# A mixer layer and sixteen experts on one core: another beginning, other fill-in steps, weight slots taken over in halves, another grouping of the last experts

## The chip, the cores and the metric

The program runs on one core of a Trainium2 chip: one TensorE (PE), VectorE (DVE), ScalarE (ACT), GpSimd (POOL), SyncE (SP) and sixteen DMA engines. The metric is device microseconds of one execution. Queues that issue DMAs are written SPq and ACTq.

## The reference

One layer on x of 512 tokens by 1024, all in float32:

```python
h = rms_norm(x, norm_mix_g)
z = h @ w_in                                   # 5648 columns
y_a = mlstm_branch(z, ...) @ w_up_a            # 4 heads, forward and backward scans, conv of width 5
y_b = diff_attention_branch(z, ...) @ w_up_b   # 4 heads, two softmaxes each
x = x + (g_a * y_a + g_b * y_b) @ w_out        # g_a, g_b: sigmoids of columns of z
h2 = rms_norm(x, norm_ffn_g)
x = x + expert_choice_ffn(h2, ...)             # 16 experts; each takes its 64 best tokens
return rms_norm(x, norm_f_g)
```

An expert is `(silu(xe @ w_gate) * (xe @ w_up)) @ w_down`, scaled by the token's affinity and added to the rows it took. Its three matrices are 1024 by 2048, 8.4 MB each, 403 MB for the sixteen.

## The kernel before

**The trunk** is everything up to the router. x comes in four tiles of 128 tokens. Each is squared on ACT (line 266) and scaled to xs; PE transposes xs into hps, ACT and DVE split it into a high part hH and a low part hL, and each product of the trunk is three float32r matmuls (lines 310 to 312), from which zps comes. The weight columns come in "heads" of 512 KB, named raw, which ACT, DVE and POOL split into two parts, sp. The first two are DQ and DK. Six small vectors (norm gains, the convolution) are loaded as rows of one tile, prow, which PE transposes to pc; a mult by pc stands in hH's evacuation and in the router's weights wr.

**What sets the order.** PE, and at the start ACT and DVE, run in the order in which the code is written (`manual_schedule`). POOL's and SP's rows are put in order by the scheduler of the language. A DMA is issued by the engine whose name stands before `dma_start`, in the order of that engine's instructions. After the matmuls of z come four mLSTM heads, in which steps of other work are run between the steps of a head ("fill-in"): for heads 0 and 1 the projections q and k of a later head, for heads 2 and 3 the generator `gate_b`, which makes the gated up-projection of the attention branch. In a head, pn are the matmuls with the scan's state, and DVE makes the row `first` that they read (line 599) and rsq (line 129).

**The experts.** The weights go through a ring of eleven slots of 2 MB (`NSLOT`), one DMA on SP for a piece of 2 MB, or two for halves of 1 MB. PIECES lists the pieces in their order; a new piece takes the slot of an older one as soon as PE has read that. A few slots are kept and not handed on (`_slots`): one holds mats (the one-hot matrices of the scatter, oa and oaT, and the results yb), one the sums acc, one the gain of the last norm. The first 23 half pieces are issued without a wait for PE, as soon as the trunk's tiles leave their space.

Expert e's passes: gate, then the down of the expert before, then up. `gather` makes xe of two experts at a time: one-hot matmuls into pg (line 1034). Two experts also share a scatter: `scatter_mats` makes the one-hot matrices (line 1047, POOL), transposes the affinities and the matrices (pa at line 1053, pt at line 1064), and `scatter` adds the results to the sums in eight passes, pg at line 1151, laid between the matmuls of another expert's up. pgate and pup are the banks of gate and up (line 1083), pd that of down (line 1167). The experts are paired (0,1) to (12,13); 14 goes alone (`no_odd`), and 15, the last, scatters nothing: its rows of the sums are picked out by one-hot matmuls px (line 1225), with pi for their numbers, its 64 rows are finished apart, and an indirect store (line 1255) writes them over out, behind four stores of the other rows (line 1245).

Of the kernel before, what the change touches and what calls it, by code (L numbers as in the profile page):

```python
# [19 lines left out]
P = 128  # L20
# [51 lines left out]
def kernel(  # L72
# [60 lines left out]
    def rsqrt_act(dst, ssq, scale, pool):  # L133
        w = pool.tile([P, 3, 4], F32, tag="rsq", name="rsq", bufs=4)
        v, u = w[:, 0, 0:dst.shape[-1]], w[:, 1, 0:dst.shape[-1]]
        ve.tensor_scalar(v, ssq, scale, EPS, op0=OP.mult, op1=OP.add)
        se.activation(u, v, AF.Sqrt)
        ve.reciprocal(dst, u)
        ve.tensor_mul(u, dst, dst)
        ve.tensor_mul(u, u, v)  # L140
        ve.tensor_scalar(u, u, -0.5, 1.5, op0=OP.mult, op1=OP.add)
        ve.tensor_mul(dst, dst, u)

# [52 lines left out]
    first_sqrt = consts.tile([P, 1], F32, name="first_sqrt")  # L196
    se.activation(first_sqrt, ident[:, 0:1], AF.Sqrt)
    prow = gt("prow", (NROW, P))
    sy.dma_start(prow[0:8], norm_mix_g[0].rearrange("(k p) -> k p", p=P))
    sy.dma_start(prow[8:16], norm_ffn_g[0].rearrange("(k p) -> k p", p=P))  # L200
    sy.dma_start(prow[16:24], conv_b[0].rearrange("(k p) -> k p", p=P))
    sy.dma_start(prow[24:64], conv_w[0].rearrange("w (k p) -> (w k) p", p=P))
    sy.dma_start(prow[64:68], mlstm_norm_g[0].rearrange("(k p) -> k p", p=P))
    sy.dma_start(prow[68:69], diff_norm_g[0:1])
# [57 lines left out]
    ss = r4.tile([P, 2, NT], F32, name="ss")  # L262
    xs = []
    for t in range(NT):
        xs.append(st_("xs", (P, D)) if t < 3 else r4.tile([P, D], F32, tag="mqk", name="xs", bufs=2))
        se.activation(xs[t], xt[t], AF.Square, accum_out=ss[:, 0, t:t + 1])
        if t % 2 == 1:
            rsqrt_act(ss[:, 1, t - 1:t + 1], ss[:, 0, t - 1:t + 1], 1.0 / D, consts)
            for i in (t - 1, t):
                if i == 2:  # L270
                    se.activation(xs[i], xt[i], AF.Copy, scale=ss[:, 1, i:i + 1])
                else:
                    ve.tensor_scalar(xs[i], xt[i], ss[:, 1, i:i + 1], None, op0=OP.mult)
# [3 lines left out]
    for ks in (range(ND - 1), range(ND - 1, ND)):  # L277
        for t in range(NT):
            for k in ks:
                pe.transpose(hps[k][:, t * P:(t + 1) * P], xs[t][:, k * P:(k + 1) * P], ident)  # L280
# [4 lines left out]
    pre[0] = sq  # L285
    for k in range(ND):
        last_evac = split_evac(hT(hH, k), hT(hL, k), hps[k], pc[:, G_MIX + k:G_MIX + k + 1])
# [425 lines left out]
    for h in range(H):  # L713
        head = mlstm_head(h)
        more = steps(lambda: mlstm_q(h + 2), lambda: mlstm_k(h + 2)) if h < 2 else gate_b
        for i, (n, m) in enumerate(((2, 2), (2, 1), (1, 1), (1, 2))):
            run(head, n)
            if (h, i) == (0, 1):
                attn_out(3)
            run(more, m)  # L720
# [253 lines left out]
    def slot_for(*key):  # L974
        n = npiece[0]
        assert PIECES[n] == key
        npiece[0] += 1
        if not NSLOT <= n < NHALVES:
            ring[SLOT_OF[n]] = mw.tile([P, 4096], F32, tag=f"w{SLOT_OF[n]}", name="w")
        return ring[SLOT_OF[n]]  # L980

    def in_halves():

        return NSLOT < npiece[0] <= NHALVES

# [32 lines left out]
    ga = consts.tile([P, 2, 1], F32, name="ga")  # L1018
    fs = consts.tile([P, 6, NT], F32, name="fs")
# [21 lines left out]
    def scatter_mats(p):  # L1041


        for t in range(NT):
            for j, q in enumerate((0, 1, 0)):
                e = 2 * p + q
# [22 lines left out]
    def first_mats():  # L1069
# [3 lines left out]
        yield from scatter_mats(0)  # L1073
# [13 lines left out]
    def up_pass(e, m, tag, ahead, behind):  # L1087
# [65 lines left out]
    def down(e, behind=nothing):  # L1153
# [4 lines left out]
        for q in range(4):  # L1158
            wt = slot_for(e, "down", q)
            src = w_down_e[0, e, q * 512:(q + 1) * 512, :].rearrange("(p i) d -> p (i d)", i=4)  # L1160
            n = 1 if (e, q) == (LAST, 3) else 2 if in_halves() else 4
            for i in range(0, 4, n):
                sy.dma_start(wt[:, i * D:(i + n) * D], src[:, i * D:(i + n) * D])
            for i in range(4):
                c = 4 * q + i
                for s, h in enumerate(order):
                    pe.matmul(pd[s * 64:(s + 1) * 64], hid_col(q, i), wt[:, i * D + h * 512:i * D + (h + 1) * 512],  # L1167
# [8 lines left out]
    def scatter(p):  # L1176
# [3 lines left out]
        for e in range(2):  # L1180
            es = slice(e * 512, (e + 1) * 512)
            for t in range(NT):
                pq = pgt((P, 512))
                scatter_mm(pq, e, t, es)
# [5 lines left out]
    def no_odd():  # L1190

        for s in range(2):
            gp.memset(yb[s * 64:(s + 1) * 64, :, (1 - s) * 512:(2 - s) * 512].bitcast(F32), 0.0)
        yield

    def others():

        for _ in range(3):
            yield
        for t in range(NT):  # L1200
            a = accs[t]
            for h in range(2):
                hs = slice(h * 512, (h + 1) * 512)
                pq = pgt((P, 512))
                scatter_mm(pq, h, t, hs)
# [8 lines left out]
    def last_rows():  # L1214

        gp.iota(tokc, pattern=[[256, NT], [1, 2]], base=0, channel_multiplier=2, allow_small_or_imprecise_dtypes=True)
        gp.tensor_tensor(pair.rearrange("p (a b) -> p a b", a=2), ident[:, 0:64].unsqueeze(1).broadcast_to([P, 2, 64]),
                         ident[:, 64:128].unsqueeze(1).broadcast_to([P, 2, 64]), op=OP.add)
        for s in range(2):
            gp.tensor_copy(gh[s * 64:(s + 1) * 64], gf[s * 64:(s + 1) * 64, s * 512:(s + 1) * 512])  # L1220
        yield
        own = [oa[:, t, CAP:2 * CAP].bitcast(F32) for t in range(NT)]
        for t in range(NT):
            for s in range(2):
                pe.matmul(px[s * 64:(s + 1) * 64, 0], own[t], accs[t][:, s * 512:(s + 1) * 512],
                          start=(t == 0), stop=(t == NT - 1))
            yield
        se.activation(xg, px[:, 0], AF.Copy)
        pi = pm.tile([P, 2], F32, tag="pt", name="pi", bufs=1)
        for s in range(2):  # L1230
            for t in range(NT):
                pe.matmul(pi[s * 64:(s + 1) * 64], own[t], tokc[:, t], start=(t == 0), stop=(t == NT - 1))
        for s in range(2):
            ve.tensor_copy(idx[s * 64:(s + 1) * 64], pi[s * 64:(s + 1) * 64, s:s + 1])
        yield
        for t in range(NT):
            a, r = accs[t], fs[:, 2, t:t + 1]
            gp.tensor_mul(a[:, 0:512], a[:, 0:512], gf[:, 0:512])
            se.activation(a[:, 0:512], a[:, 0:512], AF.Copy, scale=r)
            ve.scalar_tensor_tensor(a[:, 512:1024], a[:, 512:1024], r, gf[:, 512:1024], op0=OP.mult, op1=OP.mult)  # L1240

    def last_end(pd):
# [3 lines left out]
        ve.scalar_tensor_tensor(y, pd, ga[:, 1], xg, op0=OP.mult, op1=OP.add)  # L1246
        se.activation(sq[:, 0], y, AF.Square, scale=1.0 / 32.0, accum_out=fs[:, 5, 0:1])
# [15 lines left out]
    for e in range(NE):  # L1263
# [5 lines left out]
        else:  # L1269
            pg = up_pass(e, "gate", "pgate", nothing if e % 2 else gather(e // 2),  # L1270
                         others() if e == LAST else chain(hid_T(), scatter_mats(b // 2) if e % 2 and e > 1 else nothing))
        se.activation(sg, pg.rearrange("p a b -> p (a b)"), AF.Silu)  # L1272
        if e == LAST:
            px = pm.tile([P, 2, 512], F32, tag="pgate", name="px", bufs=1)
            pair, tokc = mats[:, 3968:4096], ohr[:, 0, 0:2 * NT].rearrange("p (t c) -> p t c", c=2)
            idx = ohr[:, 1, 0:1].bitcast(I32)
# [50 lines left out]
```

## Time and profile before

| | us |
|---|---|
| median of three runs | 1370.09 |
| lowest and highest | 1367.3, 1371.68 |
| the profiled execution | 1370.63 |
| its span | 1368.3 |
| PE busy | 1301.3 (95%) |
| DVE, ACT, POOL busy | 415.5, 304.5, 131.1 |
| DMA moved | 444.02 MB, mean 325 GB/s |

The profile is of one execution. Its times start at the span's start. Busy time is counted by engine; a wait is the idle time of an engine just before an instruction, put down to what released it. The slices of the page are 34.2 us each. The granted clock of PE is 1.00 at full speed.

### The profile page before, as it was taken

The page shows a single profiled execution, that of the slowest core. Times are in us where ns is not written, and L with a number is a line of the kernel's source. Part 1 is how long each engine was busy: PE and PEld are TensorE (multiplying, and loading weights), DVE is VectorE, ACT ScalarE, POOL GpSimd, SP SyncE. Part 2 cuts the span into 40 slices and gives each one's busy share as a digit, 9 for nine tenths or more (in the row PEclk, how much of TensorE's full clock was granted, in tenths as well). Part 3 has the DMA queues.
Part 4 walks back from the last instruction along what each step waited for, and adds up shares of the span by engine and source line. Part 5 has one row for each costly group of instructions (what it writes and reads, how often), then busy time and mean ns, then how long its engine had stood idle before and what let it go on. Part 6 is the DMA issues. An engine that isn't in the chain of part 4 may idle for free.

```text
span 1368.3 us, 16140 instructions
## 1 busy us (share of the span) xinstructions
PE 1301.3 (95%) x6566; PEld 711.8 (52%) x6566; DVE 415.5 (30%) x982; ACT 304.5 (22%) x621; POOL 131.1 (10%) x239
## 2 busy tenths in 40 slices
PE   8999999999999999999999998999899899889997
PEld 8988897888888534433433432423333242333332
DVE  5687759853443211020030020111102012010241
ACT  7676646433331010100000001000010000001030
POOL 3010212200111011000000000000000000000020
PEclk9999999999999999999999999999999999999999
DMA  7223242223478899999999999999999999999996
GB/s 205 64 64 89 81 109 62 63 77 107 134 280 344 339 425 427 427 428 427 429 428 427 428 427 428 427 428 428 428 427 429 428 427 427 427 428 427 428 427 276
DMA packets 81737, 444.02 MB, mean 325 GB/s; under 512 B 6353, under 2 KB 49431, under 8 KB 54656
## 3 DMA queue, kind: packets, MB, share of 16 engines
q1 hardware_dynamic: 79312, 438.43, 78.6%
q10 hardware_dynamic: 2240, 4.25, 1.3%
q8 instruction: 51, 0.84, 0.2%
q0 software_dynamic: 112, 0.33, 0.1%
q14 instruction: 22, 0.18, 0.0%
HBM read 440.58 MB, written 2.38 MB: 324 GB/s over the span
## 4 chain that ended last, share of the span: by engine, by line
PE 69%; DMA 22%; DVE 4%; issue 3%; ACT 2%; POOL 0%; POOLq 0%; SPq 0%; ACTq 0%; DVEq 0%
DMA w<-in_w_up_e_dram 21%; PE pgate L1083 14%; PE pup L1083 12%; PE pd L1167 7%; PE pg L1034 4%; PE zps L310 4%; PE zps L312 4%; PE zps L311 4%; PE pg L1151 3%; PE pt L1129 1%; PE bank L784 1%; PE bank L786 1%; PE bank L785 1%; PE pa L1053 1%; PE zps L352 1%
## 5 line engine op out<-in xcount | busy, mean ns | idle before, releaser
L1083 PE MATMUL pup<-w,xe 128*64 128x512 f32 x1024 | 240.1, 600 | 27.1 <-DMA w<-in_w_up_e_dram 27.1
L1083 PE MATMUL pgate<-w,xe 128*64 128x512 f32 x1016 | 243.7, 603 | 0.7 <-ACT sh L1272 0.7
L1167 PE MATMUL pd<-w,sh 128*64 128x512 f32 x1024 | 228.5, 597 | 15.4 <-DMA w<-in_w_down_e_dram 13.6
L1167 PEld LDWEIGHTS pd<-w,sh 128*64 128x64 f32 x1024 | 71.2, 137 | 162.6 <-issue 130.8
L1083 PEld LDWEIGHTS pup<-w,xe 128*64 128x64 f32 x1024 | 69.1, 136 | 165.4 <-issue 115.9
L1083 PEld LDWEIGHTS pgate<-w,xe 128*64 128x64 f32 x1016 | 63.0, 136 | 98.5 <-issue 85.2
L1146 DVE SCALAR_TENSOR_TENSOR mats<-pd,ga,mats 64x512 fp32r<-64x512 f32 x30 | 22.5, 750 | 289.1 <-ACT mats L1144 288.6
L310 PE MATMUL zps<-hH,sp 128*128 128x512 f32 x256 | 101.9, 398 | 0.8 <-DVE hL L234 0.8
L312 PE MATMUL zps<-hH,sp 128*128 128x512 f32 x256 | 100.0, 391 | 0.0
L311 PE MATMUL zps<-hL,sp 128*128 128x512 f32 x256 | 99.9, 390 | 0.0
L250 DVE TENSOR_TENSOR sp<-raw,sp 128x512 fp32r<-128x512 f32 x114 | 78.1, 688 | 54.6 <-ACT sp L249 52.0
L1034 PEld LDWEIGHTS pg<-ohr,xn 128*128 128x128 f32 x512 | 64.8, 196 | 45.4 <-issue 44.6
L249 ACT ACTIVATE sp<-raw 128x512 fp32r<-128x512 f32 x114 | 70.9, 630 | 69.5 <-PE zps L620 27.6
L1034 PE MATMUL pg<-ohr,xn 128*128 128x128 f32 x512 | 75.8, 293 | 0.2 <-DVE ohr L1027 0.2
L1284 DVE TENSOR_TENSOR sh<-sh,pup 128x512 f32<-128x512 f32 x32 | 20.6, 684 | 140.2 <-PE pup L1083 133.3
L1144 ACT ACTIVATE mats<-pd,ga 64x512 fp32r<-64x512 f32 x30 | 20.5, 683 | 191.6 <-PE pd L1167 191.3
L1038 ACT ACTIVATE xe<-pg,gff 128x128 f32<-128x128 f32 x32 | 11.8, 368 | 228.8 <-PE pg L1034 228.8
L1133 ACT ACTIVATE sh<-pt 128x512 f32<-128x512 f32 x16 | 9.6, 598 | 237.6 <-PE pt L1129 237.6
L1047 POOL TENSOR_SCALAR mats<-iota,slot 128x64 fp32r<-128x64 f32 x64 | 26.8, 444 | 313.4 <-PE pt L1064 288.2
L310 PEld LDWEIGHTS zps<-hH,sp 128*128 128x128 f32 x256 | 48.1, 188 | 10.6 <-POOL sp L284 1.0
L312 PEld LDWEIGHTS zps<-hH,sp 128*128 128x128 f32 x256 | 48.1, 188 | 10.4
L311 PEld LDWEIGHTS zps<-hL,sp 128*128 128x128 f32 x256 | 48.1, 188 | 9.5
(337 smaller groups left out, 1551.8 us busy)
## 6 DMA issues: line engine op xcount, KB each, us to landing
w<-in_w_down_e_dram SPq DMA_DIRECT2D x59, 2048.0 KB
w<-in_w_gate_e_dram SPq DMA_DIRECT2D x56, 2048.0 KB
w<-in_w_up_e_dram SPq DMA_DIRECT2D x56, 2048.0 KB
raw<-in_w_in_dram SPq DMA_DIRECT2D x44, 512.0 KB
w<-in_w_up_e_dram SPq DMA_DIRECT2D x16, 1024.0 KB
w<-in_w_gate_e_dram SPq DMA_DIRECT2D x15, 1024.0 KB
w<-in_w_down_e_dram SPq DMA_DIRECT2D x8, 1024.0 KB
raw<-in_w_out_dram SPq DMA_DIRECT2D x8, 512.0 KB
```

The costliest lines, as they stand in the source:

```text
L249: se.activation(sp[:, 0], raw, AF.Copy)
L250: ve.tensor_sub(sp[:, 1], raw, sp[:, 0].bitcast(F32))
L310: pe.matmul(zp, w[:, 1], hT(hH, k), start=(k == 0), stop=False)
L311: pe.matmul(zp, w[:, 0], hT(hL, k), start=False, stop=False)
L312: pe.matmul(zp, w[:, 0], hT(hH, k), start=False, stop=(k == ND - 1))
L1034: pe.matmul(pg, xn[t][:, c0:c0 + 255:2], ohr[:, t], start=(t == 0), stop=(t == NT - 1))
L1047: (gp if j else ve).tensor_scalar(oa[:, t, j * CAP:(j + 1) * CAP], iota, slot[:, t, e:e + 1], None, op0=OP.is_equal)
L1083: pe.matmul(pu[s * 64:(s + 1) * 64, c], xe[:, b, half:half + CAP], wt[:, c0:c0 + 512], start=(b == 0), stop=(b == ND - 1))
L1146: ve.scalar_tensor_tensor(yb[r, 1, c], src[r], ga[r, e % 2], yb[r, 0, c].bitcast(F32), op0=OP.mult, op1=OP.subtract)
L1151: pe.matmul(pq, oaT[:, v, t], yb[:, i, cols], start=(i == 0), stop=(i == 1))
L1167: pe.matmul(pd[s * 64:(s + 1) * 64], hid_col(q, i), wt[:, i * D + h * 512:i * D + (h + 1) * 512], start=(c == 0), stop=(c == 15))
L1284: ve.tensor_mul(sg[:, cols], sg[:, cols], pu[:, i])
```

## The change

Four edits. **The beginning:** the six loads of prow go from SP to ACT; SP issues DQ and DK right behind x; the table that ACT loads first is that of Exp; the reciprocal roots of the norm are made on POOL with pow; DVE takes half of a Square; the work on x goes by tiles. **The fill-in:** heads take 2, 2, 1, 1 steps, and gate_b follows where q and k have run out. **Half slots:** `OVER` lists the pieces of 1 MB that go into slots already in use, half by half: the last gate block of expert 1, the down of expert 0 and the up of expert 1; mats is kept in the first slot of these. **The last passes:** 12 is scattered alone, 13 goes with 14, and the matrices for that, own, pair and pi are made beside the down of 12, in another kept slot, "last".

```diff
 EXTRA = (0, "gate", 7)
 BLOCKS.remove(EXTRA)
+OVER = BLOCKS[2 * NSLOT:] + [(0, "down", b) for b in range(8)] + [(1, "up", b) for b in range(8)] + [None]
+BLOCKS = BLOCKS[:2 * NSLOT] + OVER
...
-    keep = {(0, "down", 0): "mats", (1, "down", 3): "acc", (12, "gate", 0): "gf"}
+    keep = {PIECES[NSLOT]: "mats", (1, "down", 3): "acc", (12, "gate", 0): "gf", (12, "gate", 1): "last"}
...
-    sy.dma_start(prow[0:8], norm_mix_g[0].rearrange("(k p) -> k p", p=P))
...
+    se.dma_start(prow[0:8], norm_mix_g[0].rearrange("(k p) -> k p", p=P))
+    se.dma_start(prow[8:16], norm_ffn_g[0].rearrange("(k p) -> k p", p=P))
+    se.dma_start(prow[16:24], conv_b[0].rearrange("(k p) -> k p", p=P))
+    se.dma_start(prow[24:64], conv_w[0].rearrange("w (k p) -> (w k) p", p=P))
+    se.dma_start(prow[64:68], mlstm_norm_g[0].rearrange("(k p) -> k p", p=P))
+    se.dma_start(prow[68:69], diff_norm_g[0:1])
+    pre = [load_head(c) for c in (DQ, DK)]
     graw = gt("graw", (P, ND, NGATE))
     sy.dma_start(graw, wi[:, MG:MG + NGATE].rearrange("(k p) c -> p k c", p=P))
-    pre = [load_head(c) for c in (DQ, DK)]
...
+    def rms(t0, t1):
+
+        v = ss[:, 0, t0:t1]
+        gp.tensor_scalar(v, v, 1.0 / D, EPS, op0=OP.mult, op1=OP.add)
+        gp.tensor_tensor(ss[:, 1, t0:t1], v, ss[:, 3, t0:t1], op=OP.pow)
...
+    se.activation(xs[3][:, 0:512], xt[3][:, 0:512], AF.Square, accum_out=ss[:, 0, 3:4])
+    ve.tensor_tensor_reduce(xs[3][:, 512:], xt[3][:, 512:], xt[3][:, 512:], 1.0, 0.0, op0=OP.mult, op1=OP.add,
+                            accum_out=ss[:, 2, 3:4])
+    gp.tensor_add(ss[:, 0, 3:4], ss[:, 0, 3:4], ss[:, 2, 3:4])
+    rms(3, 4)
...
-        more = steps(lambda: mlstm_q(h + 2), lambda: mlstm_k(h + 2)) if h < 2 else gate_b
-        for i, (n, m) in enumerate(((2, 2), (2, 1), (1, 1), (1, 2))):
+        more = [gate_b] if h > 1 else [steps(lambda: mlstm_q(h + 2), lambda: mlstm_k(h + 2)), gate_b]
+        for i, (n, m) in enumerate(((2, 2), (2, 2), (1, 1), (1, 1))):
...
-            down(b, nothing if b else first_mats())
+            down(b, last_mats() if b == LAST - 3 else nothing if b else first_mats())
...
-                         last_rows() if e == LAST else scatter(b // 2) if b % 2 else nothing)
+                         first_rows() if e == LAST else scatter(b // 2) if b % 2 and b < LAST - 2 or b == LAST - 3
+                         else nothing)
```

On ACT, the first instructions of the program before. DMAHW with a number is a semaphore of a DMA queue, the others are those of the engines; x_63, x_65, x_67 and x_69 are the four tiles of x.

```order
L760 DMA gff<-in_norm_ffn_g_dram 128x4x2
L197 ACT_TABLE_LOAD
L197 ACTIVATE first_sqrt<-ident 128x1 [waits Pool_49]
L266 ACTIVATE xs,ss<-x_63 128x1024 [waits DMAHW1_49]
L266 ACTIVATE xs,ss<-x_65 128x1024 [waits DMAHW2_49]
L137 ACTIVATE rsq<-rsq 128x2 [waits DVE_49]
L266 ACTIVATE xs,ss<-x_67 128x1024 [waits DMAHW3_49]
L266 ACTIVATE xs,ss<-x_69 128x1024 [waits DMAHW4_49]
```

And after:

```order
L187 ACTIVATE first_exp<-ident 128x1 [waits Pool_49]
L189 DMA prow<-in_norm_mix_g_dram 8x128
L190 DMA prow<-in_norm_ffn_g_dram 8x128 [waits DMAHW0_49]
L191 DMA prow<-in_conv_b_dram 8x128 [waits DMAHW2_49]
L192 DMA prow<-in_conv_w_dram 40x128 [waits DMAHW4_49]
L193 DMA prow<-in_mlstm_norm_g_dram 4x128 [waits DMAHW6_49]
L194 DMA prow<-in_diff_norm_g_dram 1x128 [waits DMAHW0_49]
L271 ACTIVATE xs,ss<-x_63 128x1024 [waits DMAHW1_49]
L271 ACTIVATE xs,ss<-x_65 128x1024
L273 ACTIVATE xs,ss<-x_67 128x1024 [waits DMAHW3_49]
L279 ACTIVATE xs,ss<-x_69 128x512
```

Six issues stand ahead of the first Square, five with a wait. DMAHW1 to DMAHW4 are, after as before, those of x's four tiles, DMAHW5 and DMAHW6 those of the heads DQ and DK; DMAHW0 is that of gff and then of a row of prow.

On POOL, at the same place, from the split of the first head on, before:

```order
L284 TENSOR_TENSOR sp<-raw,sp 128x512 [waits DMAHW4_49,Activation_49]
L284 TENSOR_TENSOR sp<-raw,sp 128x512 [waits Activation_49]
L303 TENSOR_SCALAR wr<-wr,pc 128x16 [waits DMASW0_49,DVE_49]
L303 TENSOR_SCALAR wr<-wr,pc 128x16 x7
L450 MEMSET first_305 64x512 [waits Pool_49]
L450 MEMSET first_305 64x512
L470 IOTA first_304 128x896 [waits Pool_49]
```

And after; ss holds the sums of squares and the roots:

```order
L287 TENSOR_TENSOR sp<-raw,sp 128x512 [waits DMAHW5_49,Activation_49]
L313 TENSOR_SCALAR wr<-wr,pc 128x16 [waits DMASW0_49,DVE_49]
L313 TENSOR_SCALAR wr<-wr,pc 128x16 x7
L460 MEMSET first_299 64x512 [waits Pool_49]
L460 MEMSET first_299 64x512
L480 IOTA first_298 128x896 [waits Pool_49]
L282 TENSOR_TENSOR ss<-ss 128x1 [waits DVE_49]
L460 MEMSET qk 64x512 [waits Pool_49]
L258 TENSOR_SCALAR ss<-ss 128x1 [waits Pool_49]
L460 MEMSET qk 64x512
L259 TENSOR_TENSOR ss<-ss 128x1 [waits Pool_49]
```

The last three rows of ss belong to x tile 3; they stand behind wr, the memsets of first and an iota.

On PE, the last matmuls of the program, before:

```order
L1225 MATMUL px<-acc,mats 64x512 x2
L1083 MATMUL pup<-w,xe 64x512 x2
L1232 MATMUL pi<-ohr,mats 64x2 x8
L1083 MATMUL pup<-w,xe 64x512 x20
L1129 MATMUL pt<-ident,sh 128x128 x4
L1167 MATMUL pd<-w,sh 64x512 x4
```

And after:

```order
L1266 MATMUL px<-acc,last 64x512 x2
L1108 MATMUL pup<-w,xe 64x512 x26
L1266 MATMUL px<-acc,last 64x512 x2
L1155 MATMUL pt<-ident,sh 128x128 x4
L1266 MATMUL px<-acc,last 64x512 x2
L1198 MATMUL pd<-w,sh 64x512 x4
```

px stands around the transposes of the hidden rows now, and pi has gone from here.

## Rows read from the trace of the kernel before

**Rows 1.** Lines of the page: the span; the bytes moved in 40 slices; the chain that ended last, by engine.

```profile
span 1368.3 us, 16140 instructions
...
GB/s 205 64 64 89 81 109 62 63 77 107 134 280 344 339 425 427 427 428 427 429 428 427 428 427 428 427 428 428 428 427 429 428 427 427 427 428 427 428 427 276
...
PE 69%; DMA 22%; DVE 4%; issue 3%; ACT 2%; POOL 0%; POOLq 0%; SPq 0%; ACTq 0%; DVEq 0%
```

**Rows 2.** What PE waited for from 0 to 500 us: us in total, times, longest.

```profile
PE pn L591 <- DVE first L599: 3.0, 2, 2.7
...
PE pn L591 <- DVE rsq L129: 0.6, 2, 0.5
```

**Rows 3.** Stretches of the span: length, busy time of the engines with the number of their instructions, PE's granted clock, DMA share, GB/s.

```profile
17.00:453.00 436.00, 426.22 (x2404) 369.06 (x2403) 271.30 (x679) 214.38 (x468) 68.03 (x109) 0.99 0.41 131
10.00:20.00 10.00, 8.12 (x57) 7.07 (x56) 6.46 (x18) 8.32 (x15) 5.18 (x11) 1.00 1.00 263
216.00:226.00 10.00, 9.96 (x48) 8.13 (x46) 9.87 (x29) 7.36 (x18) 3.88 (x5) 1.00 0.30 59
226.00:236.00 10.00, 6.84 (x45) 6.03 (x46) 9.16 (x28) 4.03 (x11) 3.48 (x5) 1.00 0.16 46
1340.00:1350.00 10.00, 8.37 (x33) 3.12 (x31) 1.98 (x3) 0.60 (x1) 0.00 (x0) 0.83 0.99 411
1359.00:1360.00 1.00, 1.00 (x6) 0.14 (x2) 0.00 (x0) 0.00 (x0) 0.00 (x0) 1.00 0.03 12
```

**Rows 4.** The timeline of all engines at the start: start, length, engine, line, operation, tiles; in brackets the idle time before it and what ended that.

```profile
4.71 1.06 ACT L266 ACTIVATE xs<-x 128x1024 f32<-128x1024 f32 x1 [1.91 <-DMA x<-in_x_dram]
...
5.68 0.19 ACT L266 ACTIVATION_READ_ACCUMULATOR xs<-x 128x1 f32 x1
...
9.86 1.02 SPq L183 DMA_DIRECT2D raw<-in_w_in_dram  x2
...
12.48 0.75 DVE L273 TENSOR_SCALAR xs<-x,ss 128x1024 f32<-128x1024 f32 x1
...
14.04 1.15 ACT L283 ACTIVATE sp<-raw 128x512 fp32r<-128x512 f32 x2 [0.35 <-DMA raw<-in_w_in_dram]
...
15.10 4.72 ACT L233 ACTIVATE hH<-hps,pc 128x512 fp32r<-128x512 f32 x8
...
16.70 0.47 PE L310 MATMUL zps<-hH,sp 128*128 128x512 f32 x1 [0.77 <-DVE hL L234]
```

**Rows 5.** What SP's queue waited for from 0 to 30 us.

```profile
SPq L183 <- DMA x<-in_x_dram: 1.7, 1, 1.7
...
SPq L206 <- DMA x<-in_x_dram: 1.4, 1, 1.4
```

**Rows 6.** The timeline of ACT behind the last of four DMAs that it issues.

```profile
45.11 0.58 ACTq L375 DMA_DIRECT2D rows<-rows  x1
45.80 0.63 ACT L249 ACTIVATE sp<-raw 128x512 fp32r<-128x512 f32 x1 [2.87 <-issue]
```

**Rows 7.** The timeline of POOL, at the start, and late in the span where it makes a root with pow.

```profile
14.77 2.52 POOL L284 TENSOR_TENSOR sp<-raw,sp 128x512 fp32r<-128x512 f32 x2 [11.71 <-ACT sp L283]
...
19.80 1.10 POOL L450 MEMSET first<- 64x512 f32 x2
...
20.85 0.88 POOL L470 IOTA first<- 128x896 f32 x1
...
1310.69 0.19 POOL L1210 TENSOR_TENSOR fs<-fs 128x1 f32<-128x1 f32 x1 [31.45 <-ACT gf L1207]
1310.98 0.24 POOL L1211 TENSOR_SCALAR fs<-fs 128x1 f32<-128x1 f32 x1
1311.30 0.60 POOL L1212 TENSOR_TENSOR fs<-fs 128x1 f32<-128x1 f32 x1
```

**Rows 8.** The timeline of SP's queue: the issues of the first downs and of the gate pieces after them.

```profile
463.13 16.21 SPq L1163 DMA_DIRECT2D w<-in_w_down_e_dram  x8
...
503.09 15.25 SPq L995 DMA_DIRECT2D w<-in_w_gate_e_dram  x4
```

**Rows 9.** The timeline of PE in the down of expert 0.

```profile
514.83 1.28 PE L1053 MATMUL pa<-aff,mats 128*128 128x2 f32 x10 [0.44 <-POOL mats L1047]
```

**Rows 10.** The timeline at the end.

```profile
1266.46 1.08 PE L1083 MATMUL pup<-w,xe 128*64 128x512 f32 x4 [0.58 <-DMA w<-in_w_up_e_dram]
...
1331.96 0.66 PE L1232 MATMUL pi<-ohr,mats 128*64 128x2 f32 x13
...
1347.70 12.39 PE L1167 MATMUL pd<-w,sh 128*64 128x512 f32 x56
...
1364.26 1.20 POOL L1255 DMA_INDIRECT out_dram<-sh,ohr  x1 [1.28 <-ACT sh L1253]
```

**Rows 11.** The chain that ended last, in order of time, in up and down of expert 14: start, length, engine, tile, line.

```profile
1267.54 0.67 PE pg L1151 x2
...
1291.20 1.88 PE pa L1053 x16
...
1294.95 0.59 PE pt L1064 x4
```

**Rows 12.** What PE waited for from 1183 to 1217 us.

```profile
PE pd L1167 <- DMA w<-in_w_down_e_dram: 4.1, 4, 1.2
PE pup L1083 <- DMA w<-in_w_up_e_dram: 3.7, 3, 1.2
```

More of the change, by code (lines that the diff above doesn't have):

```diff
@@ L260, in split_head @@
         return [split(raw[:, 4 * i:4 * i + 4], (4, P)) for i in range(2)]
[L262 to L273, printed above, removed]
+    ss = r4.tile([P, 4, NT], F32, name="ss")
+    gp.memset(ss[:, 3], -0.5)
+    def rms(t0, t1):
+        v = ss[:, 0, t0:t1]
+        gp.tensor_scalar(v, v, 1.0 / D, EPS, op0=OP.mult, op1=OP.add)
+        gp.tensor_tensor(ss[:, 1, t0:t1], v, ss[:, 3, t0:t1], op=OP.pow)
+    xs = [st_("xs", (P, D)) if t < 3 else r4.tile([P, D], F32, tag="mqk", name="xs", bufs=2) for t in range(NT)]
     params()
@@ L285 @@
     pre[0] = sq
+    ve.tensor_scalar(xs[2], xt[2], ss[:, 1, 2:3], None, op0=OP.mult)
+    x_T(2, range(ND - 1))
+    ve.tensor_scalar(xs[3][:, 0:512], xt[3][:, 0:512], ss[:, 1, 3:4], None, op0=OP.mult)
+    se.activation(xs[3][:, 512:], xt[3][:, 512:], AF.Copy, scale=ss[:, 1, 3:4])
+    x_T(3, range(ND - 1))
+    for t in range(NT):
+        x_T(t, (ND - 1,))
     for k in range(ND):
@@ L719 @@
                 attn_out(3)
-            run(more, m)
+            for _ in range(m):
+                while next(more[0], 0) == 0:
+                    more.pop(0)
     mp = [r4.tile([P, 2, S], F32R, tag=t, name="mp", bufs=n)
@@ L1212, in others, with last_rows, scaled, first_rows @@
             gp.tensor_tensor(r, v, fs[:, 4, 0:1], op=OP.pow)
[L1214 to L1218, printed above, removed]
+    def last_rows(t):
         for s in range(2):
[L1220 to L1226, printed above, removed]
-            yield
[L1228 to L1240, printed above, removed]
+            pe.matmul(px[s * 64:(s + 1) * 64, 0], own[:, t].bitcast(F32), accs[t][:, s * 512:(s + 1) * 512],
+                      start=(t == 0), stop=(t == NT - 1))
+    def scaled(t):
+        a, r = accs[t], fs[:, 2, t:t + 1]
+        gp.tensor_mul(a[:, 0:512], a[:, 0:512], gf[:, 0:512])
+        se.activation(a[:, 0:512], a[:, 0:512], AF.Copy, scale=r)
+        ve.scalar_tensor_tensor(a[:, 512:1024], a[:, 512:1024], r, gf[:, 512:1024], op0=OP.mult, op1=OP.mult)
+    def first_rows():
+        for t in range(2):
+            yield
+            last_rows(t)
+            scaled(t)
     def last_end(pd):
@@ L1297 @@
             rest = hid_T()
+            if e == LAST:
+                last_rows(2)
             for _ in range(3):
                 next(rest)
-            if e < LAST:
-                down(e, chain(rest, no_odd(), scatter_mats(e // 2)))
-            else:
-                last_end(down(e, rest))
+            if e == LAST:
+                last_rows(3)
+                se.activation(xg, px[:, 0], AF.Copy)
+                for t in (2, 3):
+                    scaled(t)
+            pd = down(e, rest)
+            if e == LAST:
+                last_end(pd)
 _INS = ['x', 'norm_mix_g', 'w_in', 'b_mgate', 'conv_w', 'conv_b', 'mlstm_norm_g', 'diff_lam', 'diff_norm_g',
```

152 lines of the change are left out of this document (92 added, 60 removed).

## The prediction

> **What bounds the kernel now.** I began with the page. The span of 1368.3 us, in a profiled execution of 1370.63, is nearly all PE and DMA: the chain that ended last is PE for 69% and DMA for 22%. The row of GB/s has two regimes: 62 to 134 GB/s in most of the first eleven slices of 34.2 us, and 425 to 429 from the fifteenth on [rows 1]. So the end is a sum of three things: when PE, done with the trunk, begins to free weight slots; the stream of expert weights, which then runs at a fixed rate; and the tail behind the last weight.
>
> For the trunk I read PE's waits from 0 to 500. After the start hardly anything is there: the largest is pn waiting for a DVE row, 3.0 us in two, with 0.6 behind it for rsq [rows 2]. PE is therefore the trunk's limit, and a microsecond that it loses there comes out at the end unless a wait further on takes it up. Between 17 and 453 it is busy for 426.22 of 436 us [rows 3], so of a delay at the start no more than the other 9.8 can be taken up, and 3.6 of those are pn's.
>
> **The beginning.** It adds most, and it is decided by what stands in front of ACT's first Square. Before, four Squares of x run as x lands: the first at 4.71, 1.06 us and 0.19 for its sum; then scale, transposes, the evacuation hH from 15.10 and the first matmul of the trunk at 16.70 [rows 4].
>
> After, the six small loads of the row prow stand on ACT ahead of that Square, and five of them carry a wait for an earlier load: conv_w for the one that is x tile 3, mlstm_norm for the second of the two weight heads, which SP now issues right behind x. That an issue with such a wait holds its engine is seen on SP: it stood 1.7 us at L183 and 1.4 at L206 for x [rows 5]. ACT has no such wait before, but its issues run in order with its work: one of 0.58 at 45.11, and the next activation at 45.80 after 2.87 idle [rows 6]. The step by step sum:
>
> x tile 3 lands at 9.86, which released the issue at L183 [rows 4]. The two heads, 512 KB each (0.524 MB), follow it; between 10 and 20 the trace moved 263 GB/s [rows 3], which makes 1.05/263 = 4.0 us, so 13.9. Two more issues by ACT at 0.58 [rows 6]: 15.1. Three Squares at 1.06 + 0.19 [rows 4]: 18.8. A half Square for x tile 3, about 0.7: 19.5. ACT then makes the first copy of the head, 0.58 or so of the 1.15 that two take [rows 4]: 20.1.
>
> Now POOL. Its rows are in the order shown above: between the two subs and the add that completes x tile 3's sum stand eight wr, two memsets and an iota. Before, these ran from 14.77 to 20.85 + 0.88 = 21.73 without a gap [rows 7], 6.96 us. So the add runs at 27.1; add 0.19, memset 0.55, multiply-add 0.24, memset 0.55 and pow 0.60 [rows 7] make 2.1, so 29.2. Half of the 0.75 that DVE takes for a scaled tile, 0.4, transposes of 0.2, and the 1.60 from hH's start to the first matmul [rows 4] give 31.4 against 16.70: **+14.7 us**. The rest of PE's work is in the same order.
>
> PE idles some 8 us before that. The trace has one idle spell near the end, with a granted clock of 0.83 over the next 10 us [rows 3], that is, time at the 1.2 GHz level among time at 2.4; that cost 1.7 us there, and I add **+1.7** (bounds 0 and 3.4, the double).
>
> The Exp table now loaded first saves a load of 1.28 later on ACT, which is not what PE waits for: nothing.
>
> The Trainium skill (DMA: Bandwidth & Descriptors, Issuing engines are not separate DMA queues) says that issuing from several engines saves only the time of issue, usually small. By that the move to ACT would save SP's six issues, some 2 us of issue time and none of transfer, at best; the rows on SP agree that what it stood for was landings. It is no term of the sum.
>
> **The fill-in steps.** In the mLSTM heads, gate_b's matmuls now come in where q and k have run out, and the pattern goes from 2, 1, 1, 2 to 2, 2, 1, 1. The stall that this can cover is pn's: 3.0 + 0.6 = 3.6 [rows 2]. DVE, which pn waits for, is busy 9.87 of 10 us and then 9.16, while PE falls to 6.84 in the second window [rows 3]; work for PE moved there brings DVE evacuations of its own. So not all of it comes: **−2.5**, bounds 0 and −3.6.
>
> **The half slots.** The down of expert 0 and the up of expert 1 now come in halves into slots that gate pieces leave half by half, so loading runs ahead by one half, 1.05 MB, and the SP row of eight downs (16.21 us from 463.13) can begin sooner [rows 8]. At the full rate of 428 GB/s [rows 1] that is 2.45 us. But the ring wraps at 503.09, where four gate pieces take 15.25 us to issue because each waits for PE [rows 8]: there the lead is given back to whatever PE frees late. What surely goes is PE's wait of 0.44 for POOL's mats ahead of pa at 514.83 [rows 9], since mats now gets its slot earlier. I take **−1.0**, that and a quarter of the lead, between −2.45 and +0.5 (the queue running empty once more, at the price of a wait like pa's).
>
> **The last passes.** Stream and PE end together now. The last wait of PE for an up piece ended at 1266.46; from there it works without one and is late. Its last 56 down matmuls start at 1347.70, take 12.39 and end at 1360.09 [rows 10], while DMA share is down to 0.03 at 1359 [rows 3]. Four stores of out, 2.1 MB, stand behind the weights in the same queues, 4.9 us at 428, so the last weight was there about 1354.6. PE ends 5.5 later; some 1 would do.
>
> Expert 12 now stands alone and 13 goes with 14. The scatter passes of up(14), eight pg pairs of 0.67 [rows 11], go to up(13), and pa of 1.88, pt (two of 0.59) and pi of 0.66 [rows 10] go from down(14) and up(15) to down(12), where PE stood 4.1 us for its own weights between 1183 and 1217, and 3.7 for up pieces [rows 12]. So 5.4 + 1.9 + 1.2 + 0.7 = 9.2 us leave the stretch behind the last wait, more than the 4.5 there are to win. The indirect store at 1364.26 [rows 10] also waits for the out stores, whose transfers end at 1359.5, so at most −4.4: **−4.2**, bounds −1 (where down(12) becomes late itself and the wait is put off) and −4.4.
>
> **The sum.** 14.7 + 1.7 − 2.5 − 1.0 − 4.2 = +8.7. With 1370.63 for the profiled execution that is 1379.3; it stands 0.5 over the median of 1370.09, so **1379** is the forecast. What a measurement here can tell from no change is 0.3%, 4.1 us.
>
> **The rivals.**
> A: ACT is not held by the small loads' waits, so the Squares start as x lands, but POOL's order stands. The first head lands at 11.9; copies end at 12.5, POOL's rows at 19.4, the add, multiply-add and pow at 21.5, and the first matmul runs at 23.7: +7.0, and +1.7 for the clock. With −7.7 for the other edits that is +1.0, **1371**: the same. For it: no row shows ACT held by a landing ahead of an issue. Against: SP is held so [rows 5]. Chance 0.08.
> The Trainium skill (DMA: Bandwidth & Descriptors, Anatomy of one DMA) says that DMA engines don't wait for semaphores; a wait happens on the sequencer of the issuing engine, before dispatch. By that ACT is held, and A is out; SP's rows agree, and no run here shows it of ACT.
> B: the start costs nothing, because the waits are met when they come up and the memsets and iotas on POOL slip behind the pow; the other edits give −7.7, **1362.4**: faster. For it: POOL's rows before x tile 3 are short ones that could run early; against: the order is fixed in the program. Chance 0.10.
> C, slower still: the start as forecast, and the gains of the MoE part are eaten where the ring wraps: each half there is an issue of its own, and if the queue is empty once more PE's wait of 1.2 at a piece comes back, so −1.0 turns into +0.5 and −4.2 into −1. 16.4 − 2.5 + 0.5 − 1.0 = +13.4, **1383.5**. Decided by whether PE waits for gate(2) at 503 to 520. Chance 0.08.
>
> The forecast itself has 0.74, with a range of its own of 1374 to 1384: DQ and DK landing 1.5 earlier and the full 3.6 on one side, double the clock and no fill-in on the other. With A that gives a range of 1370 to 1385, which leaves out B and little of C. Faster by over 0.3%: 0.10 for B and 0.01 of A, 0.11; within 0.3%: 0.07; slower: 0.82.
>
> **What would show it.** In the profile after, PE's first matmul of the trunk at about 31 with its wait put down to xs or ss; ACT's first Square near 15 behind a wait for a raw load; on POOL, iota ahead of the add; a granted clock under 1 between 30 and 45. pn's wait on DVE near 230 smaller than 3.0; no POOL chain before pa; the last down matmuls ending at most 1.5 us behind their weight, and pa, pt and px gone from the last two experts. I am wrong if the first Square starts before 9, or if the first matmul of the trunk runs before 25.

## The result, and the profile after

The changed kernel takes 1384.82 us (median of 4 runs, 1383.72 to 1385.22) beside 1370.05 for the kernel before: ratio 1.0101, 95% interval 1.0088 to 1.0115. It is slower, as forecast, by 14.8 us where the sum said 8.7. 1384.82 is just inside the stated range of 1370 to 1385, but outside the forecast's own 1374 to 1384; rival C's 1383.5 is nearest.

The page after, the lines of [rows 1]:

```profile
span 1383.2 us, 16155 instructions
...
GB/s 157 93 77 62 61 108 77 75 78 80 134 186 366 355 416 387 427 427 427 427 426 426 426 428 425 428 426 426 427 427 427 427 426 427 426 428 426 427 421 318
...
PE 64%; DMA 29%; DVE 3%; ACT 2%; POOL 1%; issue 1%; SPq 0%; POOLq 0%; ACTq 0%; DVEq 0%
```

DMA's share of the chain grew from 22 to 29%, and two things are new in the row of GB/s: 416 and 387 where the stream was already at 425 and 427 before, and 426 or 427 in most slices that had 427 or 428.

The timeline at the start, all engines, as [rows 4] and [rows 7]:

```profile
12.97 0.26 ACTq L194 DMA_DIRECT2D prow<-in_diff_norm_g_dram  x1
...
13.28 1.06 ACT L271 ACTIVATE xs<-x 128x1024 f32<-128x1024 f32 x1 [10.48 <-DMA graw<-in_w_in_dram]
...
24.94 0.88 POOL L480 IOTA first<- 128x896 f32 x1
25.80 0.18 POOL L282 TENSOR_TENSOR ss<-ss 128x1 f32<-128x1 f32 x1
...
27.39 0.56 POOL L259 TENSOR_TENSOR ss<-ss 128x1 f32<-128x1 f32 x1
...
29.14 2.61 PE L268 MATMUL hps<-ident,xs 128*128 128x128 f32 x11 [7.30 <-DVE xs L291]
...
31.40 0.77 PE L320 MATMUL zps<-hH,sp 128*128 128x512 f32 x1
```

Both links of the forecast are there. ACT stands 10.48 us with its first Square behind prow's last issue (the bracket names graw only because that load, which uses the semaphore of x's first tile again, landed last, at 13.1). POOL's add for x tile 3 stands behind the iota. The first matmul of the trunk runs at 31.40, which is the forecast to the tenth, in part by luck (below).

Stretches after, with the granted clock in the third column from the right:

```profile
15.00:21.00 6.00, 3.60 (x17) 3.50 (x18) 3.83 (x7) 3.16 (x8) 5.19 (x6) 0.50 0.84 258
17.00:30.00 13.00, 5.30 (x25) 4.97 (x26) 4.38 (x6) 2.23 (x6) 11.71 (x22) 0.63 0.38 118
30.00:40.00 10.00, 10.00 (x39) 8.36 (x38) 8.46 (x17) 8.88 (x18) 1.13 (x3) 0.75 0.14 39
40.00:60.00 20.00, 20.00 (x134) 18.37 (x133) 10.20 (x24) 10.73 (x23) 0.43 (x1) 1.00 0.37 103
```

Behind its wait of 7.30 PE worked at the 1.2 GHz level for a part of the second stretch: the seven trunk matmuls behind the first one, from 31.97 to 34.53, take 0.63 us each, not 0.40, and the tenth starts at 35.24, 3.84 us after the first. In the kernel before the tenth starts 2.16 us after the first: 1.7 lost, as forecast. The clock had fallen once already, to 0.50 from 15 to 21, behind waits of 2.76 and 2.79; that cost nothing, since PE then waited its 7.30 all the same.

What SP's queue waited for from 465 to 580 us, then in the kernel before from 500 to 525:

```profile
SPq L1016 <- PE pd L1198: 6.5, 1, 6.5
...
SPq L1016 <- PE pt L1089: 6.2, 1, 6.2
```

```profile
SPq L995 <- PE pt L1064: 9.7, 1, 9.7
```

These waits are for slots that PE reads late. The third gate piece of expert 2 is issued 6.9 us behind the second now, and the fourth 6.2 behind the third. Before, the third followed after 1.7 and only the fourth waited.

PE's end in the timeline:

```profile
1373.38 1.08 PE L1198 MATMUL pd<-w,sh 128*64 128x512 f32 x4 [0.18 <-DMA w<-in_w_down_e_dram]
...
1379.20 1.20 POOL L1294 DMA_INDIRECT out_dram<-sh,idx  x1 [1.87 <-DMA out_dram<-acc]
```

PE's last matmuls now wait for their weight and end 1.1 us behind it, at 1374.46; before they ended at 1360.09 [rows 10], 5.2 behind the last weight, which landed at 1354.86 by the semaphores in the trace. The indirect store waits 1.87 for the out stores, which it did not before [rows 10].

### The profile page after: what moved, and what is told of

Its sections match the earlier page's. It is cut to its first block, busy times and chain, and to the rows that moved or that the text cites. A ratio compares the mean times of both kernels' runs of the same rounds, so it can differ in the third digit from the quotient of the medians.

```text
span 1383.2 us, 16155 instructions
## 1 busy us (share of the span) xinstructions
PE 1304.5 (94%) x6566; PEld 714.3 (52%) x6566; DVE 418.9 (30%) x978; ACT 301.1 (22%) x618; POOL 136.8 (10%) x248
## 4 chain that ended last, share of the span: by engine, by line
PE 64%; DMA 29%; DVE 3%; ACT 2%; POOL 1%; issue 1%; SPq 0%; POOLq 0%; ACTq 0%; DVEq 0%
DMA w<-in_w_up_e_dram 24%; PE pgate L1108 12%; PE pup L1108 11%; PE pd L1198 5%; PE pg L1058 4%; PE zps L320 4%; PE zps L321 4%; PE zps L322 4%; PE pg L1178 2%; DMA w<-in_w_gate_e_dram 2%; DMA w<-in_w_down_e_dram 1%; PE pt L1155 1%; PE bank L796 1%; PE bank L798 1%; PE bank L797 1%; PE zps L362 1%
## 5 line engine op out<-in xcount | busy, mean ns | idle before, releaser
L1198 PE MATMUL pd<-w,sh 128*64 128x512 f32 x1024 | 228.6, 595 | 16.4 <-DMA w<-in_w_down_e_dram 15.6
L1173 DVE SCALAR_TENSOR_TENSOR mats<-pd,ga,mats 64x512 fp32r<-64x512 f32 x26 | 19.5, 750 | 244.5 <-ACT mats L1171 244.0
L1171 ACT ACTIVATE mats<-pd,ga 64x512 fp32r<-64x512 f32 x26 | 17.7, 682 | 168.1 <-PE pd L1198 167.8
L1070 POOL TENSOR_SCALAR mats<-iota,slot 128x64 fp32r<-128x64 f32 x56 | 23.3, 442 | 292.6 <-PE pt L1089 269.1
```

The costliest lines, as they stand in the source:

```text
L1070: (gp if j else ve).tensor_scalar(oa[:, t, j * CAP:(j + 1) * CAP], iota, slot[:, t, e:e + 1], None, op0=OP.is_equal)
L1173: ve.scalar_tensor_tensor(yb[r, 1, c], src[r], g[r], yb[r, 0, c].bitcast(F32), op0=OP.mult, op1=OP.subtract)
L1198: pe.matmul(pd[s * 64:(s + 1) * 64], hid_col(q, i), wt[i // 2][:, c0:c0 + 512], start=(c == 0), stop=(c == 15))
```

## Experiments

All are timed against the kernel before on the same chip, whose median was 1370.55 to 1370.63 there.

### The beginning: what holds ACT, and what holds POOL

**Prow's loads back on SP**, the rest as changed:

```diff
-    se.dma_start(prow[0:8], norm_mix_g[0].rearrange("(k p) -> k p", p=P))
+    sy.dma_start(prow[0:8], norm_mix_g[0].rearrange("(k p) -> k p", p=P))
...
```

> The changed kernel with one edit: the six loads of prow go back to SP, ahead of DQ and DK. Theory (ACT is held by these loads' waits, and then POOL's order holds x tile 3): ACT's first Square goes back from 13.28 to about 4.7, but POOL's add for tile 3 now stands behind the first head's subs, four memsets, an iota, eight wr and another iota; with the head landing near 13.9 as in the kernel before, the add runs near 23.7 and the first matmul of the trunk near 26.9 instead of 31.40, so 1380 us (1378 to 1382). Rival 1 (only ACT's hold counts, POOL's order is harmless): first matmul near 17, 1369. Rival 2 (only POOL's order counts): no gain, 1384 to 1386.

1380.15 us (1.0064, 1.0047 to 1.0081). Its timeline:

```profile
4.55 1.06 ACT L271 ACTIVATE xs<-x 128x1024 f32<-128x1024 f32 x1 [1.75 <-DMA x<-in_x_dram]
...
22.78 0.19 POOL L282 TENSOR_TENSOR ss<-ss 128x1 f32<-128x1 f32 x1
...
26.73 0.78 PE L320 MATMUL zps<-hH,sp 128*128 128x512 f32 x1
```

The Square is back at 4.55, but the add still stands in POOL's queue until 22.78: one of the two links alone gives back 4.7 us.

**POOL in the written order**, prow still on ACT:

```diff
-    start_order.enter_context(tc.manual_schedule(engines={mybir.EngineType.DVE, mybir.EngineType.Activation}))
+    start_order.enter_context(tc.manual_schedule(engines={mybir.EngineType.DVE, mybir.EngineType.Activation, mybir.EngineType.Pool}))
```

> The changed kernel with one edit: at the start POOL too runs in the written order, so the add, multiply-add and pow of x tile 3 stand ahead of the first head's subs, wr, memsets and iotas. Theory: the first Square stays near 13.3, pow for tile 3 is done near 19.8 instead of 27.9, and the first matmul of the trunk runs near 23 instead of 31.40; PE's idle spell of 7.3 us goes and with it most of the 2 us at the low clock: 1374.5 us (1373 to 1377). Rival 1 (only ACT's hold counts): 1384 to 1386. Rival 2 (only POOL's order counts): first matmul near 17, 1369.

1376.25 us (1.0038, 1.0025 to 1.005), 1.8 more than the number expected, inside its range:

```profile
12.95 1.06 ACT L271 ACTIVATE xs<-x 128x1024 f32<-128x1024 f32 x1 [10.15 <-DMA prow<-in_conv_w_dram]
...
19.37 0.54 POOL L259 TENSOR_TENSOR ss<-ss 128x1 f32<-128x1 f32 x1
...
23.47 0.47 PE L320 MATMUL zps<-hH,sp 128*128 128x512 f32 x1 [0.56 <-DVE hL L224]
```

**Both edits:**

> Both edits of the two runs beside it: prow's loads on SP, POOL in the written order. Theory: x tile 3 is scaled on DVE near 12.5, but ACT's half of it stands behind the two copies of the first head, which lands near 13.9, so the first matmul runs near 17.8 instead of 31.40 and the clock stays up: 1369.5 us (1368 to 1371.5). Rival (the root by pow on POOL and the halved Square cost time themselves): first matmul after 20, 1372 or more.

1371.66 us (1.0008, 0.9998 to 1.0018), a little over the range: the first matmul ran at 18.60. Two links in a row, each seen alone and both together: rivals 1 and 2 fall. Together they are worth 13.2 us.

**The old beginning** in the changed kernel:

> The changed kernel with the whole beginning of the kernel before; fill-in, half slots and last passes stay. Theory (the beginning costs 14.7 us and about 2 for the clock, and nothing of it is given back): 1368 us (1366.5 to 1370), PE 2.2 ahead of the kernel before at the first expert by the fill-in, and the rest of the loss of the changed kernel (about +1.4 in the half slots, +2 in the stream, -4.1 in the last passes) unchanged. Rival (the other three edits are worth the 7.7 us that I forecast for them): 1362.5 us.

1368.98 us (0.9985, 0.9976 to 0.9995). So the beginning costs 1384.82 − 1368.98 = 15.8 us. Of these, 2.7 stay when both links are out: the first matmul of the trunk runs at 18.60 there and at 16.33 with the old beginning. The other three edits together are worth 1.6 us, not 7.7.

### Where the 7.7 went: half slots and last passes

**Half slots alone:**

```diff
-    keep = {(0, "down", 0): "mats", (1, "down", 3): "acc", (12, "gate", 0): "gf"}
+    keep = {PIECES[NSLOT]: "mats", (1, "down", 3): "acc", (12, "gate", 0): "gf"}
...
+OVER = BLOCKS[2 * NSLOT:] + [(0, "down", b) for b in range(8)] + [(1, "up", b) for b in range(8)] + [None]
```

> The kernel before with the half slots alone (mats kept in the first slot that is taken over). Theory from the traces (the place of mats: it keeps the slot that the third gate piece of expert 2 had before, so that piece waits for the second and third half of expert 0's down): gate(2) pieces 0 and 1 land some 1.7 us earlier, pieces 2 and 3 some 1.5 to 3.5 later than before, and the end is 1.5 us later, 1372 us (1371 to 1374). Rival (my forecast: the lead of one half is kept in part): 1369.5 us.

1370.69 us (1.0000, 0.9992 to 1.0009): no change, between theory and rival and outside the range. Its stretches from 515 to 530 and from 650 to 1100 us, and then the first of them in the kernel before:

```profile
515.00:530.00 15.00, 15.00 (x75) 5.68 (x76) 2.87 (x10) 2.56 (x4) 3.33 (x8) 1.00 0.96 354
650.00:1100.00 450.00, 420.10 (x1973) 157.39 (x1971) 63.35 (x133) 34.18 (x55) 22.50 (x48) 1.00 1.01 428
```

```profile
515.00:530.00 15.00, 15.00 (x76) 5.90 (x78) 2.87 (x10) 2.56 (x4) 3.93 (x10) 1.00 1.00 424
```

354 GB/s from 515 to 530, where it was 424: there the queue runs empty. By the semaphores in the trace, piece 0 of gate(2), the first of its four, landed 1.2 us earlier than before and piece 3, the last, 2.5 later.

**Mats in the second slot that is taken over**, made four steps later, with the old beginning:

```diff
-    keep = {PIECES[NSLOT]: "mats", (1, "down", 3): "acc", (12, "gate", 0): "gf", (12, "gate", 1): "last"}
+    keep = {PIECES[NSLOT + 1]: "mats", (1, "down", 3): "acc", (12, "gate", 0): "gf", (12, "gate", 1): "last"}
...
-        for _ in range(4):
+        for _ in range(8):
```

> The changed kernel with the old beginning (1368.98 measured) and mats in the second slot that is taken over, made four steps later: the third gate piece of expert 2 then gets the slot of gate(1) and the first half of down(0), which are read first. Theory (the place of mats decides): gate(2) piece 2 is issued 2 us or more earlier, the lead is kept, 1366 us (1364.5 to 1367.5). Rival (the ring is simply too short, wherever mats lies): no change, 1369.

1366.67 us (0.9971, 0.9960 to 0.9981), against 1368.98 with the first slot. The same stretch of this run, and then of the run with the old beginning:

```profile
515.00:530.00 15.00, 15.00 (x78) 6.18 (x79) 2.86 (x10) 2.56 (x4) 3.33 (x8) 1.00 0.99 403
```

```profile
515.00:530.00 15.00, 15.00 (x74) 5.29 (x75) 2.24 (x6) 2.56 (x4) 3.31 (x8) 1.00 0.95 366
```

All four pieces of gate(2) land 3.7 us earlier than before here; with mats in the first slot piece 3 lands 1.4 later. The place of mats cost 2.3 us. The edit has two parts, but the slot shows by itself: piece 2 is issued 3.4 us behind piece 1, and 6.9 behind it with mats in the first slot.

**Last passes alone**, and **fill-in with last passes:**

> The kernel before with the last passes alone. Theory: PE ends its last down matmul about 1.1 us behind the last weight instead of 5.2, less 0.5 that comes back in the tail: 1367 us (1366 to 1368.5). Rival (the matrices made beside the down of 12 delay the stream there, because the ring is one slot smaller): 1370 or more, with the last weight landing 2 us later than before.

> The kernel before with fill-in and last passes, without the half slots and the new beginning. Theory: the 2.2 us that PE gains by the fill-in reach the stream, since gate(2) finds its slots as before: 1364.8 us (1363.5 to 1366.5). Rival (the stream gives the lead back at the wrap in any case): 1367, as with the last passes alone.

1370.59 us (1.0001, 0.9992 to 1.0010) and 1368.49 (0.9986, 0.9978 to 0.9995). Both are outside their ranges. So the fill-in gives 2.1, as the theory had it, and the last passes nothing. Yet PE ends 1.1 us behind its last weight in both. The weights themselves came later, and not at one place, as the rival of the first run had it. In each kernel with the last passes and the moved ring the stream fell back against the kernel before by some 0.011 us a piece, all along: a packet of 16 KB took 617.0 ns between 650 and 1100 us (the mean of some 11,700 packets in a trace), beside 616.0 in the kernel before and with the half slots alone. What these kernels share there is no work, but memory: three new constants (gl, tokc, idx) take 128 bytes of each partition, and the ring moves from byte 34656 to 34784.

**The ring moved, the work unchanged:**

```diff
     fs = consts.tile([P, 6, NT], F32, name="fs")
+    spare = consts.tile([P, 32], F32, name="spare")
+    gp.memset(spare, 0.0)
```

> The kernel before with an unused row of 128 bytes among the constants, so that every slot of the ring lies 128 bytes higher, as it does in all kernels here with the last passes. In their traces a packet of 16 KB takes 617.0 ns on average between 650 and 1100 us, in the kernel before and in the one with half slots alone 616.0, and the stream falls back 0.011 us per 2 MB piece. Theory (the place of the slots does it): 617.0 ns, the last up piece of expert 14 lands 1.7 us or more later against the first, 1372.4 us (1371.5 to 1373.5). Rival (it is the work of the last passes): 616.0 ns, 1370.6 us.

1372.22 us (1.0019, 1.0008 to 1.0029), and 617.0 ns a packet. (The trunk's tiles, which use the ring's bytes before it does, move along.) The stretch from 650 to 1100 us:

```profile
650.00:1100.00 450.00, 423.61 (x1987) 159.53 (x1986) 63.75 (x134) 34.18 (x55) 22.52 (x48) 1.00 1.01 427
```

**The ring put back**, the three constants in a kept slot, in the kernel with mats in the second slot:

```diff
-    gl = consts.tile([P, 3, 1], F32, name="gl")
-    tokc = consts.tile([P, NT, 3], F32, name="tokc")
-    idx = consts.tile([P, 1], I32, name="idx")
...
+            tokc = kg[:, 2 * D:2 * D + 12].rearrange("p (t c) -> p t c", t=NT)
+            gl = kg[:, 2 * D + 16:2 * D + 19].rearrange("p (a b) -> p a b", a=3)
+            idx = kg[:, 2 * D + 20:2 * D + 21].bitcast(I32)
```

> The kernel with the old beginning and mats in the second slot (1366.67), with three small constants of the last passes put into a kept slot, so that the ring lies where it lay before. Theory (the place of the slots costs 0.011 us a piece): packets of 16 KB back at 616.0 ns, 1364.6 us (1363.5 to 1365.5). Rival: 617.0 ns and 1366.7 us, no change.

1364.38 us (0.9958, 0.9944 to 0.9971), and 616.0 ns. This version beats both kernels: 6.2 us under the kernel before and 20.4 under the changed one. **And in the one with the last passes alone:**

> The last passes alone, with the three small constants in a kept slot, so that the ring lies where it lay in the kernel before. Theory (the last passes are worth what I forecast at PE's end, and the moved ring gave it back): packets of 16 KB at 616.0 ns, PE's last down matmul about 1.1 us behind the last weight, 1368.2 us (1367 to 1369.3) beside 1370.59 with the ring moved. Rival (PE's lag at the end did not set the time of the kernel before): 1370 to 1371.

1369.00 us (0.9989, 0.9980 to 0.9997), at 616.0 ns and with PE 1.1 us behind its last weight: 1.6 us gained, two fifths of the forecast; the expected range holds it.

### A third beginning

Prow's transpose and copies behind the scaling of x tiles 0 to 2, prow on SP, POOL as written, in the fastest version:

```diff
     x_T(2, range(ND - 1))
+    params()
     ve.tensor_scalar(xs[3][:, 0:512], xt[3][:, 0:512], ss[:, 1, 3:4], None, op0=OP.mult)
```

> As the run beside it, but with a third beginning: the changed kernel's, with prow's loads on SP, POOL in the written order, and prow's transpose and copies only after x tiles 0 to 2 are scaled. Theory (in the beginning with both edits it was DVE that came late, because pc's copies stood ahead of the scaling and waited for PE): DVE's half of the Square of tile 3 ends near 10.6 instead of 13.4, and the first matmul of the trunk runs near 16 instead of 18.6: 1364 us (1362.5 to 1365.5). Rival (the first weight head, landing near 11.8, and POOL's split of it hold the first matmul): 17.5 or later, 1365.5 or more.

1367.10 us (0.9974, 0.9965 to 0.9983): a miss, and not by the rival's reason.

```profile
12.01 1.16 ACT L285 ACTIVATE sp<-raw 128x512 fp32r<-128x512 f32 x2 [1.98 <-DMA raw<-in_w_in_dram]
...
14.13 0.23 DVE L233 COPY pc<-tps 128x69 f32<-128x69 f32 x1 [2.70 <-PE tps L232]
...
15.23 0.86 DVE L291 TENSOR_SCALAR xs<-x,ss 128x512 f32<-128x512 f32 x1
```

The last row's tile was ready to be scaled at 12.1, when pow ended, but pc's copy stood ahead of it on DVE and waited 2.70 us for PE, which had the transposes of three tiles to do first. The stall moved with the copy.

## Why the prediction was right or wrong

| edit | forecast | measured |
|---|---|---|
| beginning, with the clock | +16.4 | +15.8 |
| fill-in | −2.5 | −2.1 |
| half slots | −1.0 | 0.0 alone, +0.5 beside the others |
| last passes | −4.2 | 0.0; −1.6 with the ring put back |
| sum | +8.7 | +14.2 of 14.8 |

(Measured: by the medians above; +0.5 is 1368.98 less 1368.49, from two chips. The 0.6 that is left lies in the kernel before: 1370.05 in the four runs beside the changed kernel, 1370.55 to 1370.63 in the 17 to 32 runs beside each experiment.)

The direction was right, and so was the term that decides it. The sum was 6.1 us short, mainly in the two terms of the experts. That the stated range still held the result, with 0.2 us to spare, is luck. Its ends were not added up from what I named for them either: double the clock and no fill-in make 1383.2, not 1384, and the heads 1.5 earlier with the full fill-in 1376.4, not 1374.

**The beginning** was right in its mechanism, its two links and its size; A and B fall by ACT's 10.48 us and by the runs that take one link out. That 31.40 came out to the tenth is luck, since two misses cancelled. Pow ended at 27.95, not 29.2: the heads landed sooner, and the first Square ran at 13.28, not 15.1. From there to the first matmul it took 3.45 us, not 2.2: the scaling alone took 1.10 on DVE where I had 0.4. The Trainium skill (DMA: Bandwidth & Descriptors, Anatomy of one DMA) puts the wait for a semaphore on the sequencer of the issuing engine; what SP's rows showed before, the 10.48 us of ACT now show for ACT. **The clock** fell as forecast, and cost what the sum had. I took its price from one dip; the other one of that trace, 0.66 from 440 to 450, would have given 3.4. **The fill-in** came nearly whole by the medians, but the rows show only part of it. PE's wait at pn, 3.0 and 0.6 before [rows 2], is 2.7 with the fill-in, in three short ones (here with the old beginning):

```profile
PE pn L592 <- DVE first L600: 2.7, 3, 1.4
```

PE's busy time from 200 to 300 us, first in the kernel before, then with the old beginning:

```profile
200.00:300.00 100.00, 96.35 (x508) 81.20 (x507) 78.46 (x230) 50.35 (x124) 17.95 (x29) 1.00 0.25 69
```

```profile
200.00:300.00 100.00, 97.35 (x511) 82.29 (x510) 80.35 (x229) 50.04 (x123) 18.51 (x29) 1.00 0.26 69
```

That is 1.0 of the 2.1. The other half lies where the trunk ends, and its cause stays open: from 440 to 450 the granted clock is 0.66 before and 0.83 with the old beginning, but 0.72 where mats took the second slot, and there the first gather of expert 0 begins as early (451.67 beside 451.62; before 453.81).

**The half slots** failed at "there the lead is given back": I sized it as a loss of the lead alone, −1.0 being left; what came, 0.0 and +0.5, is at my upper bound of +0.5. I had the right place and didn't ask which slot each piece gets. Mats took over the slot that piece 2 of gate(2) had before; that piece was left with the slot of the second and third half of down(0), which PE reads later. That costs 2.3 us by the run that moves mats. Rival C had the place and the empty queue, but neither this reason nor the sign: between 500 and 620 us PE waits for no weight, before or after. It is the stream that falls behind.

**The last passes** failed at "the last weight was there about 1354.6": the reading was good (1354.86), but I held the stream fixed and only moved PE. PE's lag fell as forecast, from 5.2 to 1.1, yet the gain was 0.0, outside my bounds of −1 and −4.4. Three things gave it back; the first is shown by runs, the others are read from traces. The ring's new place costs 1.6 to 2.3 us (1372.22 beside 1370.59; 1366.67 beside 1364.38). The changed kernel also loads the last expert's up and down in halves of 1 MB, which the list of edits does not name: with the ring in place the first of the sixteen DMA engines to finish is 0.6 us later at the last weight, against the kernel before, than it was at the last up piece of expert 14. No run has these halves alone, so that they are the cause is not shown. And the indirect store waits 1.87 for the out stores, the limit that I named; from PE's end to the span's end it took 8.2 us before and 8.8 now. A lag of 5.2 was moreover that one execution's: with the ring moved it was 2.9 in the kernel before, and 4.0 with the half slots alone. One of my signs could not come true: px stays in the last expert, as PE's order already showed.

What stays open: in two executions with the same trunk its end differs by up to 1.9 us (the first down of expert 0 starts 1.1 earlier with the last passes alone and 0.8 later with the ring moved alone). A difference of one or two microseconds is therefore read from medians here, not from two traces.

## What to carry to other kernels

A DMA issue that is moved to a compute engine takes its wait along, and the whole queue of that engine stands behind it; look at the order on each engine for rows without a reason to be first, since a scheduler put memsets ahead of the one small add on which PE waited. In a ring, ask of each piece which older piece's slot it gets and when that is read for the last time, above all where a slot is kept. A new constant moves everything behind it in memory, so time a layout change by itself before its price is put down to the work.

## What the runs showed of the hardware that I had not expected

The place of a buffer in a partition sets the rate of a saturated stream: 128 bytes higher, a packet of 16 KB takes 617.0 ns in place of 616.0 (0.17%), in all nine kernels here with the ring at 34784 beside all five with it at 34656, and the difference is 1.6 to 2.3 us in the end. The two places are 224 and 96 bytes past a multiple of 256. The Trainium skill (DMA: Bandwidth & Descriptors, How a descriptor splits into AXI transactions) says that the first transaction of a descriptor which doesn't start at such a multiple starts at the multiple below, and that the bytes before the start are fetched for nothing and still cost beats of 32 bytes. With a packet taken as one descriptor that is 519 beats against 515, an estimate of 0.8% worked out from that page: the direction agrees, the size is a fifth. The page speaks of bytes that are fetched, while these loads write the ring, so that this is the cause is not shown. A ring at a multiple of 256 wasn't tried.

PE's clock fell in the third beginning too. PE's timeline there, and the stretch behind it:

```profile
16.14 1.42 PE L267 MATMUL hps<-ident,xs 128*128 128x128 f32 x11 [2.04 <-DVE xs L291]
18.12 0.71 PE L320 MATMUL zps<-hH,sp 128*128 128x512 f32 x1 [0.56 <-DVE hL L224]
18.63 0.63 PE L321 MATMUL zps<-hL,sp 128*128 128x512 f32 x1
```

```profile
18.00:22.00 4.00, 3.88 (x10) 3.10 (x11) 4.00 (x7) 4.00 (x8) 3.83 (x11) 0.57 0.82 259
```

A granted clock of 0.57 over 4 us is 3.4 us at the 1.2 GHz level, 1.7 lost: as much as behind the wait of 7.30 in the changed kernel. With both edits of the beginning PE stood 1.48 at the same transposes and the granted clock stayed at 1.00 from 14 to 22. With POOL in the written order the clock fell as well, behind waits of 2.87 and 2.56, but was up again when the first matmul of the trunk ran at 23.47:

```profile
14.00:20.00 6.00, 3.31 (x15) 3.11 (x16) 3.20 (x9) 3.88 (x11) 3.99 (x8) 0.50 0.86 262
...
23.00:27.00 4.00, 3.53 (x16) 2.96 (x17) 4.00 (x7) 4.00 (x9) 3.88 (x10) 1.00 0.47 135
```

So the price of a stall at the start is not its length alone: it counts what PE has to do until the clock is up again.
